# Low parts of the MLP weights: accumulating DMA onto negated high parts in place of a VectorE subtraction

## The chip, the cores and the metric

The kernel runs on one core of one Trainium2 chip. The metric is the device time of one execution in microseconds (us); for the kernel before it is the median of 3 runs.

## The reference

A two-layer decoder trunk over x of 512 tokens by 1024 features, in float32. Layer 0 mixes tokens by differential attention, layer 1 by a chunkwise mLSTM; each mixer is followed by a squared-ReLU MLP, and a final RMSNorm ends it.

```
h = x
for layer in range(DEPTH):                       # DEPTH = 2
    mix = diff_attention(...) if layer % 2 == 0 else mlstm_mixer(...)
    h = h + mix
    h = h + sqrelu_mlp(rmsnorm(h, mlp_norm[layer]), mlp_w1[layer], mlp_w2[layer])
return rmsnorm(h, final_norm)

def sqrelu_mlp(h, w1, w2):                       # w1: 1024 x 4096, w2: 4096 x 1024
    return jnp.square(jax.nn.relu(h @ w1)) @ w2
```

## The kernel before, in words

Activations lie transposed, features on the 128 partitions and the 512 tokens along the row. Every dense product is made of three TensorE passes in a rounded format (fp32r): each operand is split into a high part, its rounded copy, and a low part, the float32 value minus the high part. `mm3` (L296 to L299) issues high x high (L297), high weight x low activation (L298) and low weight x high activation (L299).

The weights are cut into 192 units of 128 x 1024 float32 (two of them 128 x 1056), in the order in which TensorE uses them (`PLAN`). Each entry of `PLAN` is the name of a matrix and its parts; the names are `a_in`, `a_out`, `w1_0`, `w2_0`, `m_in`, `m_out`, `w1_1`, `w2_1`. The two MLPs use 64 units each: for `w1`, four units that serve four output tiles together and 28 of one output tile, for `w2` two units for each of 8 output tiles in each of two halves. A unit is 24 matmuls of 128 x 512.

`issue()` (from L263) brings in one unit. SP issues the load of `raw` from DRAM (L278), ScalarE rounds it into `whi` (through the helper `act`, whose instructions all bear L230), and VectorE subtracts to give `wlo` (L282). `raw`, `whi` and `wlo` have three buffers each. `unit()` is called as TensorE turns to unit u, and issues what is missing up to unit u+2; so the high and low parts of u+2 are written into the buffers that unit u-1 has just left.

TensorE's order is the order of the program, with other work put in at counted steps (`tick`, `after`). The instructions of the other engines are ordered by the scheduler of the language from their dependencies and its own estimates; each engine then runs its instructions in that fixed order and waits where it must.

Around the MLPs the other work is this. At the end of each mixer the output projection (`outproj`) finishes the 8 tiles of h; each is added by VectorE (L499), split by `operand` into `x_xh` (ScalarE) and `x_xl` (VectorE, L409), squared by ScalarE, and the squares are summed into `acc` by GpSimd (L420). Eleven steps into the MLP `token_scale` splits `acc` (L424) and TensorE sums it over partitions (L431, L432). In the `w1` part ScalarE applies Relu, VectorE squares (L754), and both split the result into `u_uh` and `u_ul` (L424). In the `w2` part VectorE scales the result and adds it to h (L766, L767). GpSimd's own DMAs are those of the attention bias (`skew` L533, `bias` L540) and a few constants.

Of the kernel before, what the change touches and what calls it, by code (L numbers as in the profile page):

```python
# [14 lines left out]
AF = mybir.ActivationFunctionType  # L15
ALU = mybir.AluOpType
# [63 lines left out]
def _plan():  # L80

    units = []

    def group(m, cols):
        for k2 in range(KT // 2):
            units.append((m, [(k, c, P) for k in (2 * k2, 2 * k2 + 1) for c in cols]))

    def ntile(m, c, k0=0):
        units.append((m, [(k0 + k, c, P) for k in range(KT)]))

    def vpair(m, c, extra=None):
        for k4 in range(2):
            parts = []
            for k in range(4 * k4, 4 * k4 + 4):
                parts.append((k, c, 256))
                if extra is not None:
                    parts.append((k, extra, 2 * MH))
            units.append((m, parts))

    def outproj(m, wide):  # L100
        order = [(k, n * P, P) for k, n in out_order(wide)]
        units.extend((m, order[i : i + 8]) for i in range(0, len(order), 8))

    def mlp(m1, m2):
        group(m1, [0, P, 2 * P, 3 * P])
        for half in range(2):
            for n in range(16 * half, 16 * half + 16):
                if n >= 4:
                    ntile(m1, n * P)
            for n in range(KT):  # L110
                ntile(m2, n * P, 16 * half)
                ntile(m2, n * P, 16 * half + 8)

    group("a_in", [0, D, P, D + P])
    vpair("a_in", 2 * D)
    for h in range(2, AH):
        ntile("a_in", h * P)
        ntile("a_in", D + h * P)
        if h % 2 == 1 and h < AH - 1:
            vpair("a_in", 2 * D + (h // 2) * 256)  # L120
    vpair("a_in", 2 * D + 3 * 256)
    outproj("a_out", A_WIDE)
    mlp("w1_0", "w2_0")
    vpair("m_in", D, 3 * D)
    for h in range(MH):
        ntile("m_in", h * P)
        ntile("m_in", 512 + h * P)
    for v in range(1, MH):
        vpair("m_in", D + v * 256)
        for n in GATES_AFTER[v]:  # L130
            ntile("m_in", 2 * D + n * P)
    outproj("m_out", M_WIDE)
    mlp("w1_1", "w2_1")
    return units


PLAN = _plan()
# [24 lines left out]
def trunk(ctx: ExitStack, tc, xT, wgt, wgt2, cols, rows, rel, consts, outT):  # L162
    nc = tc.nc
# [10 lines left out]
    def nm(s):  # L174
        return f"{s}_{next(names)}"
# [26 lines left out]
    vec = nc.vector  # L202
    pool = nc.gpsimd

    def asf(t):
        return t.bitcast(F32)
# [5 lines left out]
    def behind(ins, before):  # L212
        tc.add_manual_dep(
            ins.ins, before.ins.name,
            mybir.DependencyInfo(mybir.DependencyClass.NoSync, mybir.DependencyReason.DATA),
            reason="table order",
        )

    def tables(name):
        if loaded["set"] != name:  # L220
            load = nc.scalar.preload_act_table_set(name)
            for use in loaded["uses"]:
                behind(load, use)
            loaded.update(set=name, load=load, uses=[load])

    def act(out, x, func, **kw):
        name = {AF.Exp: LNSET, AF.Ln: LNSET, AF.Sigmoid: SGSET}.get(func)
        if name:
            tables(name)
        ins = nc.scalar.activation(out, x, func, **kw)  # L230
        if name:
            behind(ins, loaded["load"])
            loaded["uses"].append(ins)
# [29 lines left out]
    def issue():  # L263
        u = state["next"]
        state["next"] += 1
        w = WIDTHS[u]
        raw = wp.tile([P, UW], F32, tag="raw", name=nm("raw"))
        if w == 1024:
            src = wgt[u - state["wide"]]
        else:  # L270
            src = wgt2[state["wide"]]
            state["wide"] += 1
        hi = wp.tile([P, UW], F32R, tag="whi", name=nm("whi"))
        lo = wp.tile([P, UW], F32R, tag="wlo", name=nm("wlo"))
        parts = 2 if u < 2 else 1
        for i in range(parts):
            c = slice(i * w // parts, (i + 1) * w // parts)
            nc.sync.dma_start(raw[:, c], src[:, c])  # L278
        for i in range(parts):
            c = slice(i * w // parts, (i + 1) * w // parts)  # L280
            act(hi[:, c], raw[:, c], AF.Copy)
            vec.tensor_tensor(lo[:, c], raw[:, c], asf(hi[:, c]), op=ALU.subtract)  # L282
        ready[u] = (hi, lo)

    used = iter(range(len(PLAN)))
# [1 line left out]
    def ahead(u):  # L287
        while state["next"] <= min(u, len(PLAN) - 1):
            issue()
# [814 lines left out]

    arrive(0)
    issue()
    arrive(1)
    issue()
    for k in range(KT // 2, KT):
        nc.sync.dma_start(h[k], xT[k])  # L1110
# [77 lines left out]
```

## Time and profile before

| | |
|---|---|
| median of 3 runs | 1211.18 us (1209.6 to 1211.62) |
| the profiled execution | 1211.02 us, span 1209.2 us |
| mean granted TensorE clock | 0.992 |
| DMA moved | 111.15 MB, mean 92 GB/s |
| first MLP, second MLP (from the span's start) | 254.6 to 612, 838.7 to 1190 us |

Times within a profile count from the start of its span. PE is TensorE's matmuls, PEld its weight loads, DVE VectorE, ACT ScalarE, POOL GpSimd, SP the engine that issues most DMAs. A row of a group gives line, engine and operation, what is written from what, how often, busy time and mean nanoseconds of one, and then the engine's idle time before them with what ended it. A row of the timeline gives start and duration in us, and in brackets the idle time before it and its releaser. The matmuls are pipelined, so 0.40 us rows start about 0.23 us apart.

### The profile page before, as it was taken

The numbers are of one execution on the slowest core, as the hardware profiler recorded it, in microseconds if no ns is written. First come the engines' busy times: TensorE is split into PE (matmuls) and PEld (weight loads), VectorE is DVE, ScalarE is ACT, GpSimd is POOL, SyncE is SP. The second block draws the span as 40 slices with busy tenths as digits, with TensorE's granted clock in tenths as the row PEclk, the third lists the DMA queues.
The fourth block names the chain that finished last, engine by engine and source line by source line (L and its number), as shares of the span: only waits on it lengthen the run. The fifth ranks groups of instructions, "written<-read, shape, count | busy, mean of one in ns | idle before, by whom it ended". The sixth has DMA issues, their size and how long they took to land.

```text
span 1209.2 us, 14346 instructions
## 1 busy us (share of the span) xinstructions
PE 1175.9 (97%) x5610; PEld 975.0 (81%) x5610; DVE 684.5 (57%) x1063; ACT 524.2 (43%) x845; POOL 168.7 (14%) x157
## 2 busy tenths in 40 slices
PE   8899999999999999999999899999999999999996
PEld 5778888888888888888887789878888888888885
DVE  6789897575433344434469857666544333444444
ACT  5567776454331223433344546655433122433221
POOL 4432332130000000001101312213000000000011
PEclk9999999999999999999999999999999999999998
DMA  6622222222322223232321221222232323222222
GB/s 197 197 70 70 79 79 71 76 99 87 103 89 90 102 87 104 87 103 89 98 93 64 89 69 53 70 87 87 92 100 87 104 88 103 90 91 101 87 70 70
DMA packets 33123, 111.15 MB, mean 92 GB/s; under 512 B 3967, under 2 KB 6034, under 8 KB 33056
## 3 DMA queue, kind: packets, MB, share of 16 engines
q1 hardware_dynamic: 30288, 103.38, 25.9%
q0 software_dynamic: 1648, 5.29, 1.6%
q10 hardware_dynamic: 1120, 1.57, 0.4%
q8 instruction: 44, 0.72, 0.2%
q14 instruction: 23, 0.19, 0.1%
HBM read 108.11 MB, written 4.74 MB: 93 GB/s over the span
## 4 chain that ended last, share of the span: by engine, by line
PE 84%; DVE 8%; ACT 3%; DMA 2%; issue 2%; POOL 1%; DVEq 0%; SPq 0%; ACTq 0%; POOLq 0%
PE bank L298 24%; PE bank L299 24%; PE bank L297 24%; PE bank L330 1%; PE bank L329 1%; PE bank L331 1%; DVE wlo_wlo L282 1%; DMA raw_raw<-wgt 1%; DVE tmp_tmp L827 1%; PE bank L623 1%; PE bank L624 1%; ACT kh_kh L230 1%; PE bank L656 1%; ACT whi_whi L230 1%; DVE e_e L643 0%
## 5 line engine op out<-in xcount | busy, mean ns | idle before, releaser
L282 DVE TENSOR_TENSOR wlo_wlo<-raw_raw,whi_whi 128x1024 fp32r<-128x1024 f32 (+1 forms) x194 | 243.1, 1253 | 269.2 <-ACT whi_whi L230 268.9
L230 ACT ACTIVATE whi_whi<-raw_raw 128x1024 fp32r<-128x1024 f32 (+1 forms) x194 | 203.6, 1049 | 403.4 <-PE bank L298 358.9
L299 PE MATMUL bank<-x_xh,wlo_wlo 128*128 128x512 f32 x768 | 306.0, 398 | 1.1 <-DVE wlo_wlo L282 1.1
L298 PE MATMUL bank<-x_xl,whi_whi 128*128 128x512 f32 x768 | 305.0, 397 | 1.1 <-DVE x_xl L409 1.1
L297 PE MATMUL bank<-x_xh,whi_whi 128*128 128x512 f32 x768 | 303.3, 395 | 2.0 <-ACT whi_whi L230 1.5
L299 PE MATMUL bank<-u_uh,wlo_wlo 128*128 128x512 f32 x496 | 197.1, 397 | 0.0
L298 PE MATMUL bank<-u_ul,whi_whi 128*128 128x512 f32 x496 | 196.3, 396 | 0.0
L297 PE MATMUL bank<-u_uh,whi_whi 128*128 128x512 f32 x496 | 193.7, 391 | 0.0
L297 PEld LDWEIGHTS bank<-x_xh,whi_whi 128*128 128x128 f32 x768 | 146.9, 191 | 35.3 <-ACT whi_whi L230 2.2
L298 PEld LDWEIGHTS bank<-x_xl,whi_whi 128*128 128x128 f32 x768 | 145.0, 189 | 34.3 <-DVE x_xl L409 1.8
L299 PEld LDWEIGHTS bank<-x_xh,wlo_wlo 128*128 128x128 f32 x768 | 144.9, 189 | 34.1 <-DVE wlo_wlo L282 2.1
L420 POOL TENSOR_TENSOR acc_acc<-acc_acc,tmp_tmp 128x512 f32<-128x512 f32 x34 | 53.6, 1576 | 717.8 <-ACT tmp_tmp L230 717.1
L297 PEld LDWEIGHTS bank<-u_uh,whi_whi 128*128 128x128 f32 x496 | 94.6, 191 | 22.0
L298 PEld LDWEIGHTS bank<-u_ul,whi_whi 128*128 128x128 f32 x496 | 93.1, 188 | 22.1
L299 PEld LDWEIGHTS bank<-u_uh,wlo_wlo 128*128 128x128 f32 x496 | 93.1, 188 | 20.2
L766 DVE TENSOR_TENSOR tmp_tmp<-bank,rs_rs 128x512 f32<-128x512 f32 x31 | 21.4, 692 | 107.1 <-PE bank L299 107.1
L230 ACT ACTIVATE u_uh<-tmp_tmp 128x512 fp32r<-128x512 f32 x64 | 40.4, 632 | 79.1 <-DVE tmp_tmp L754 78.9
L329 PE MATMUL bank<-whi_whi,x_xh 128*128 128x256 f32 (+1 forms) x256 | 72.7, 284 | 0.0
L330 PE MATMUL bank<-wlo_wlo,x_xh 128*128 128x256 f32 (+1 forms) x256 | 72.1, 282 | 0.0
L331 PE MATMUL bank<-whi_whi,x_xl 128*128 128x256 f32 (+1 forms) x256 | 72.0, 281 | 0.0
L424 DVE TENSOR_TENSOR u_ul<-tmp_tmp,u_uh 128x512 fp32r<-128x512 f32 x64 | 44.3, 692 | 39.1 <-ACT u_uh L230 39.1
L329 PEld LDWEIGHTS bank<-whi_whi,x_xh 128*128 128x128 f32 x256 | 48.3, 189 | 0.5
(242 smaller groups left out, 1493.3 us busy)
## 6 DMA issues: line engine op xcount, KB each, us to landing
raw_raw<-wgt SPq DMA_DIRECT2D x188, 512.0 KB, 3.5
skew<-frd POOLq DMA_DIRECT2D x8, 320.0 KB, 6.7
bias_bias<-skew POOLq DMA_DIRECT2D x8, 256.0 KB, 3.1
outT<-h SPq DMA_DIRECT2D x6, 256.0 KB, 2.3
raw_raw<-wgt SPq DMA_DIRECT2D x2, 528.0 KB, 3.6
h<-xT ACTq DMA_DIRECT2D x4, 256.0 KB, 6.8
raw_raw<-wgt SPq DMA_DIRECT2D x4, 256.0 KB, 8.7
h<-xT SPq DMA_DIRECT2D x4, 256.0 KB, 6.4
```

The costliest lines, as they stand in the source:

```text
L230: ins = nc.scalar.activation(out, x, func, **kw)
L282: vec.tensor_tensor(lo[:, c], raw[:, c], asf(hi[:, c]), op=ALU.subtract)
L297: mm(ps, whi, x[0], start=first, stop=False)
L298: mm(ps, whi, x[1], start=False, stop=False)
L299: mm(ps, wlo, x[0], start=False, stop=last)
L329: mm(ps, xh, hi[:, c], start=k == 0, stop=False)
L330: mm(ps, xh, lo[:, c], start=False, stop=False)
L331: mm(ps, xl, hi[:, c], start=False, stop=k == KT - 1)
L420: pool.tensor_tensor(acc, acc, s, op=ALU.add)
L424: (eng or vec).tensor_tensor(lo, src, asf(hi), op=ALU.subtract)
L623: mm(ps[m][:, o : o + n], q2[m][:, qs], kh[m][:, :n], start=True, stop=False)
L766: vec.tensor_tensor(y, p, rs2, op=ALU.mult)
```

## The change

In `issue()`, for units whose matrix name begins with "w" (the 128 units of the two MLPs), the subtraction on VectorE is left out. ScalarE makes a second copy of `raw`, with scale -1, into `lo` in the rounded format, and GpSimd issues a DMA that reads the unit's weights again from DRAM and adds them onto `lo`. The other 64 units keep the subtraction.

```
             act(hi[:, c], raw[:, c], AF.Copy)
-            vec.tensor_tensor(lo[:, c], raw[:, c], asf(hi[:, c]), op=ALU.subtract)
+            if PLAN[u][0][0] == "w":
+
+                act(lo[:, c], raw[:, c], AF.Copy, scale=-1.0)
+                nc.gpsimd.dma_start(lo[:, c], src[:, c], accum_op=ALU.add)
+            else:
+                vec.tensor_tensor(lo[:, c], raw[:, c], asf(hi[:, c]), op=ALU.subtract)
         ready[u] = (hi, lo)
```

## Prediction

> **What bounds the kernel now.** I read the page's busy table first, then the table of stretches over the two MLP stages, the costliest groups, the waits of TensorE, and last the timeline of one unit.
>
> ```profile
> PE 1175.9 (97%) x5610; PEld 975.0 (81%) x5610; DVE 684.5 (57%) x1063; ACT 524.2 (43%) x845; POOL 168.7 (14%) x157
> ```
>
> ```profile
> 254.60:612.00 357.40, 357.40 (x1544) 290.79 (x1543) 150.25 (x174) 117.06 (x150) 12.73 (x9) 1.00 0.30 97
> 838.70:1190.00 351.30, 351.30 (x1538) 286.75 (x1537) 149.93 (x171) 110.63 (x141) 10.54 (x7) 1.00 0.27 89
> ```
>
> The second fence holds the two MLP stages; the columns after the length are the busy times of PE, its weight loads, VectorE (DVE), ScalarE (ACT) and GpSimd (POOL), then the granted clock, the DMA share and GB/s. TensorE is busy for the whole of both, 357.40 + 351.30 = 708.7 us, at clock 1.00, while VectorE is busy 300 us of it. In the stages that the change touches, VectorE is not the bound.
>
> ```profile
> L282 DVE TENSOR_TENSOR wlo_wlo<-raw_raw,whi_whi 128x1024 fp32r<-128x1024 f32 (+1 forms) x194 | 243.1, 1253 | 269.2 <-ACT whi_whi L230 268.9
> L230 ACT ACTIVATE whi_whi<-raw_raw 128x1024 fp32r<-128x1024 f32 (+1 forms) x194 | 203.6, 1049 | 403.4 <-PE bank L298 358.9 <-issue 29.0 <-DMA raw_raw<-wgt 7.1
> ```
>
> ```profile
> PE bank L299 <- DVE wlo_wlo L282: 1.1, 2, 0.6
> PE bank L298 <- DVE x_xl L409: 1.1, 2, 0.8
> ```
>
> The 194 subtractions are 192 units, the first two in halves. The second fence is from TensorE's waits over the whole run (us, times, longest): it stood 1.1 us for a low part and 1.1 us for an operand's low part. ACT's 358.9 us of waiting for `L298` is the wait for a buffer: the high part of unit u+2 goes into the buffer that unit u-1 leaves.
>
> ```profile
> 305.24 1.06 ACT L230 ACTIVATE whi_whi<-raw_raw 128x1024 fp32r<-128x1024 f32 x1 [2.03 <-PE bank L298]
> 306.20 0.58 ACT L230 ACTIVATE tmp_tmp<-bank 128x512 f32<-128x512 f32 x1
> 310.78 1.06 ACT L230 ACTIVATE whi_whi<-raw_raw 128x1024 fp32r<-128x1024 f32 x1 [1.96 <-PE bank L298]
> 316.33 1.06 ACT L230 ACTIVATE whi_whi<-raw_raw 128x1024 fp32r<-128x1024 f32 x1 [1.96 <-PE bank L298]
> 306.33 1.23 DVE L282 TENSOR_TENSOR wlo_wlo<-raw_raw,whi_whi 128x1024 fp32r<-128x1024 f32 x1 [2.40 <-ACT whi_whi L230]
> 316.79 0.40 PE L299 MATMUL bank<-x_xh,wlo_wlo 128*128 128x512 f32 x1
> ```
>
> One unit takes 316.33 - 310.78 = 5.55 us. The unit whose high part starts at 305.24 has its low part at 306.33 + 1.23 = 307.56, and TensorE first reads that at 316.79: 9.2 us of slack.
>
> **What is removed.** The MLPs have 2 x 64 = 128 of the 192 units (4 + 28 of `w1` and 32 of `w2` each). 128 subtractions of 1.23 us, 157 us, leave VectorE. None is on the path in the MLP windows, where TensorE had no idle time, so this is worth 0 to 2.2 us (all of both waits above, though nothing shows that they belong to these units). I take 0.
>
> **What ACT gains.** 128 negated copies of the same shape as the high part: 128 x 1.06 = 136 us, on an engine that is busy 117.06 + 110.63 = 228 us of 708.7; it comes to 51%. ACT starts the next instruction 0.96 us after a high part (305.24 to 306.20), so the copy runs from about 306.20 to 307.26, as early as the subtraction ended. The Relu at 306.20 moves back a microsecond, and VectorE's square, which stood behind the subtraction, is free sooner; the result is read a stage later. Cost 0, hidden by TensorE's unit. The raw tile, which the subtraction used to free, is freed by the copy at about the same time, so SP's queue of loads isn't moved.
>
> **What the DMA gains.** Each of the 128 units reads its 512 KB of weights from DRAM a second time and adds them onto the low part in SBUF, issued by POOL. The trace has no accumulating DMA; its nearest rows are POOL's plain loads into SBUF, POOL's copies within DRAM, and SP's loads of this size.
>
> ```profile
> raw_raw<-wgt SPq DMA_DIRECT2D x188, 512.0 KB, 3.5
> skew<-frd POOLq DMA_DIRECT2D x8, 320.0 KB, 6.7
> bias_bias<-skew POOLq DMA_DIRECT2D x8, 256.0 KB, 3.1
> ```
>
> ```profile
> q1 hardware_dynamic: 2592, 9.44, 29.6%
> raw_raw<-wgt SPq DMA_DIRECT2D x18, 512.0 KB, 3.4
> ```
>
> ```profile
> L540 POOL DMA_DIRECT2D bias_bias<-skew x8: 567/590/592, 40.6 to 163.3; - x8
> ```
>
> The last number of the first fence's rows is us from issue to landing; the second fence is the DMA table of the stretch from 300 to 400 us. There 18 loads took 29.6% of 16 engines for 100 us: 29.6 / 18 = 1.64 us of all engines for one 512 KB pass. POOL itself works 0.59 us per issue.
>
> Time to landing, from below: a plain POOL load, 3.1 us for 256 KB and half a pass more, 3.9 us. From above: at the rate of the slowest kind, `skew`, 6.7 x 512 / 320 = 10.7, plus 1.64 for the raw load that the same copy releases and that shares the engines: 12.4 us. An accumulate has to read its destination too, so I take two passes and the raw load beside it: 3.9 + 1.64 + 1.64 = 7.2 us. That is near the `bias` row, which like this one goes from DRAM into SBUF. The DMA may start at 307.26 and is wanted at 316.79, 9.5 us later; 7.2 fits with 2.3 us to spare. Below nothing it can't go, since TensorE has no idle time to give back here.
>
> Engine time: two passes and the raw load are 3 x 1.64 = 4.9 us in a unit of 5.55. It fits as long as the accumulate takes less than 5.55 - 1.64 = 3.9 us, or 2.4 passes. The forecast hangs on this.
>
> The row says 1.64 us for one pass of a copy. The Trainium skill, Collectives: The Full Stack, section "The bandwidth ceiling: the fold count and why AG ≠ RS ≠ AR", holds that a reducing DMA is slower not because of the addition but because it reads two sources, and gives 32.35 against 62.28 GB/s, 1.93 times a copy. By it the accumulate would take an estimated 3.2 us; no run here shows it yet.
>
> **What POOL gains.** A DMA waits in POOL's order for its negated copy, and what stands behind it are the sums of squares (`L420`) that the token scale needs at the start of each MLP.
>
> ```profile
> 243.30 8.76 POOL L420 TENSOR_TENSOR acc_acc<-acc_acc,tmp_tmp 128x512 f32<-128x512 f32 x5 [5.72 <-ACT tmp_tmp L230]
> 245.40 1.05 ACT L230 ACTIVATE whi_whi<-raw_raw 128x1024 fp32r<-128x1024 f32 x1
> 247.47 1.72 DVE L282 TENSOR_TENSOR wlo_wlo<-raw_raw,whi_whi 128x1024 fp32r<-128x1024 f32 x1
> 249.12 3.49 DVE L409 SCALAR_TENSOR_TENSOR x_xl<-h,colt,x_xh 128x512 fp32r<-128x512 f32 x2
> 255.09 0.39 PE L299 MATMUL bank<-x_xh,wlo_wlo 128*128 128x512 f32 x1
> 257.02 1.38 POOL L420 TENSOR_TENSOR acc_acc<-acc_acc,tmp_tmp 128x512 f32<-128x512 f32 x1 [0.86 <-ACT tmp_tmp L230]
> 259.10 0.69 DVE L424 TENSOR_TENSOR sl_sl<-acc_acc,sh_zeros 128x512 fp32r<-128x512 f32 x1 [0.15 <-ACT sh_zeros L230]
> 262.49 0.39 PE L432 MATMUL bank<-sl_sl,ones_d 128*128 128x512 f32 x1
> ```
>
> At the first MLP's start the first unit's high part is at 245.40, its negated copy would end near 247.4, and TensorE reads the low part at 255.09. POOL has five additions in a row there, to 252.06. Between two of them the DMA is issued one addition late, 247.4 + 1.75 = 249.15, and lands 5.5 us (were no raw load beside it) to 7.2 us later, 254.7 to 256.4: a stall of 0 to 1.3 us. Behind all five it lands at 252.06 + 7.2 = 259.3, a stall of 4.2. VectorE's order was planned with this unit's low part ahead of two operands (249.12) that the program names earlier, so work is placed when it is ready; I take the first case, near its upper end because the raw load is released by the same copy: 1 us. The last addition (257.02) may be put off by one issue, 0.6 us, with 262.49 - 259.79 = 2.7 us in hand: 0.
>
> ```profile
> 827.53 1.06 ACT L230 ACTIVATE whi_whi<-raw_raw 128x1024 fp32r<-128x1024 f32 x1 [2.14 <-issue]
> 829.86 1.80 POOL L420 TENSOR_TENSOR acc_acc<-acc_acc,tmp_tmp 128x512 f32<-128x512 f32 x1 [2.82 <-ACT tmp_tmp L230]
> 839.16 0.40 PE L299 MATMUL bank<-x_xh,wlo_wlo 128*128 128x512 f32 x1
> ```
>
> At the second MLP's start the units come more slowly; even behind the addition, at 831.66, a DMA of 7.2 us lands at 838.9, ahead of 839.16: 0.
>
> **Sum.** Removed 0, ACT 0, DMA 0, POOL +1. The profiled execution took 1211.02 us, 1.8 us of it outside its span of 1209.2, and is 0.16 below the median of 1211.18. With +1 the median becomes 1212.2. A measurement of this kernel tells about 0.2% (2.4 us) from no change, so this is no change.
>
> **Rivals.** *The DMA engines become the bound.* For it: nothing here shows an accumulate, three passes in place of two are enough, and the loads come in bursts. Against it: at two passes the engines stay under 90%. It decides from 2.4 passes on. At three passes a unit takes 4 x 1.64 = 6.56 us, 1.01 more than now, times 128: +129 us, 1340. At four it is 1550. With the upper landing bound instead, three units (as many as there are buffers) take copy, DMA and use in turn, (307.26 - 305.24 + 12.4 + 5.55) / 3 = 6.66 us, which is 1.11 x 128 = +142 and 1353.
>
> *POOL's order puts the first DMA behind all five additions.* Steady state hidden, +4.2 at one place: 1215.4. For it: those additions stand earlier in the program. Against it: the VectorE order above.
>
> *VectorE's lighter load frees something.* All of both waits give -2.2 us, 1209.0, still within 0.2%; to be faster than that a chain of VectorE outside the MLPs would have to start sooner. Against it: VectorE is under half busy in both MLPs, so it carries no backlog out of them.
>
> **How the numbers follow.** Forecast, within 2.4 us of before: 0.53, its own range 1209 to 1213.6. DMA engines or landing too slow: 0.31, of which about half is under +142 us. POOL's order: 0.12. Faster by over 0.2%: 0.04. So faster 0.04, same 0.53, slower 0.12 + 0.31 = 0.43. The range from 1208 to 1353 takes in the forecast, POOL's order, half of the slow DMA and most of the rest, 0.83.
>
> **What would show it.** Right: both MLP stretches again with PE busy all of their length, no TensorE wait for the accumulating DMA but at about 255 us, landing near 7 us, DMA share in the MLPs near 0.9. Wrong: TensorE waiting for low parts in every unit, the DMA share near 1.0 (engines) or well below (latency), or a wait of 4 us at the first MLP alone (POOL). The forecast falls if the accumulate takes more than 3.9 us of engine time or lands later than 9.5 us.

## The result, and the profile after

The kernel after takes 1215.45 us (median of 5 runs, 1214.85 to 1216.94) against 1211.18 for the kernel before in the same series (5 runs, 1209.58 to 1212.02). The ratio is 1.0041, with a 95% interval of 1.0026 to 1.0056, some 5 us (the medians differ by 4.3): a small loss, but the whole interval lies beyond the 0.2% that the prediction had set as its border. The profiled execution is the fastest of the five, 1214.85 us, with a span of 1213.1.

The page of the kernel after: busy times, SP's queue with its share of the 16 engines, two groups, and the DMA issues with the us to landing.

```profile
PE 1178.8 (97%) x5610; PEld 976.7 (81%) x5610; DVE 532.8 (44%) x935; ACT 637.6 (53%) x973; POOL 275.3 (23%) x285
...
q1 hardware_dynamic: 30288, 103.38, 29.4%
...
L285 POOL DMA_DIRECT2D wlo_wlo<-wgt x128 | 111.0, 867 | 572.7 <-ACT wlo_wlo L230 555.8
...
L230 ACT ACTIVATE wlo_wlo<-raw_raw 128x1024 fp32r<-128x1024 f32 x128 | 133.9, 1046 | 0.0
...
raw_raw<-wgt SPq DMA_DIRECT2D x188, 512.0 KB, 5.3
wlo_wlo<-wgt POOLq DMA_DIRECT2D x128, 512.0 KB, 7.6
```

The change did what it says: VectorE lost 152 us (684.5 to 532.8), ScalarE gained 113, GpSimd 107. The accumulating DMA lands in a median of 7.6 us, and the plain load beside it now takes 5.3 instead of 3.5. The two MLP stages of the kernel after, with the columns as before:

```profile
254.60:612.00 357.40, 355.69 (x1532) 288.68 (x1532) 76.67 (x110) 171.47 (x212) 65.12 (x72) 1.00 0.87 189
838.70:1190.00 351.30, 351.22 (x1521) 285.69 (x1520) 75.09 (x108) 165.28 (x204) 63.77 (x70) 1.00 0.87 184
```

The DMA share went from 0.30 and 0.27 to 0.87, and TensorE is still busy for nearly the whole of both. Of the first, 1.71 us are missing. TensorE's waits in the kernel after name them:

```profile
PE bank L304 <- DMA wlo_wlo<-wgt: 1.7, 1, 1.7
```

One wait, for one accumulating DMA. Its place is the start of the first MLP; these are rows of the timeline of the kernel after, GpSimd, ScalarE and TensorE:

```profile
244.98 8.22 POOL L425 TENSOR_TENSOR acc_acc<-acc_acc,tmp_tmp 128x512 f32<-128x512 f32 x5 [5.72 <-ACT tmp_tmp L230]
253.14 0.95 POOL L285 DMA_DIRECT2D wlo_wlo<-wgt  x1
...
247.07 1.05 ACT L230 ACTIVATE whi_whi<-raw_raw 128x1024 fp32r<-128x1024 f32 x1
248.03 0.71 ACT L230 ACTIVATE x_xh<-h,colt 128x512 fp32r<-128x512 f32 x1
248.64 0.62 ACT L230 ACTIVATE tmp_tmp<-h 128x512 f32<-128x512 f32 x1
249.27 0.72 ACT L230 ACTIVATE x_xh<-h,colt 128x512 fp32r<-128x512 f32 x1
249.90 0.61 ACT L230 ACTIVATE tmp_tmp<-h 128x512 f32<-128x512 f32 x1
250.42 1.05 ACT L230 ACTIVATE wlo_wlo<-raw_raw 128x1024 fp32r<-128x1024 f32 x1
...
256.30 0.39 PE L302 MATMUL bank<-x_xh,whi_whi 128*128 128x512 f32 x1
...
258.60 0.50 PE L304 MATMUL bank<-x_xh,wlo_wlo 128*128 128x512 f32 x1 [1.68 <-DMA wlo_wlo<-wgt]
```

GpSimd runs all five additions and only then issues the DMA, and ScalarE makes the negated copy four instructions behind the high part. Two matmuls of 0.23 us stand ahead of the first reader, so that was due at 256.30 + 0.47 = 256.77 and came at 258.60, 1.83 us late. The second unit's reader comes another 0.33 us late, found by matching TensorE's instructions of both traces one by one.

The same matching shows 1.65 us of lag by 59 us of the span, long before the first accumulating DMA. It is the clock. In the kernel before:

```profile
28.00:36.00 8.00, 5.62 (x24) 4.03 (x23) 5.21 (x7) 3.48 (x5) 1.92 (x4) 1.00 0.35 106
54.00:64.00 10.00, 9.16 (x39) 7.94 (x40) 7.63 (x28) 4.81 (x18) 1.82 (x3) 0.83 0.35 113
```

and in the kernel after:

```profile
28.00:36.00 8.00, 5.77 (x18) 4.42 (x19) 4.50 (x7) 3.10 (x5) 2.76 (x6) 0.79 0.40 124
54.00:64.00 10.00, 8.76 (x31) 7.65 (x32) 7.44 (x28) 4.70 (x16) 1.79 (x3) 0.66 0.31 107
```

The granted clock, third number from the end, fell to 0.79 and 0.66 over these stretches, where before it was 1.00 and 0.83. So of the 3.9 us between these two spans only 2.2 belong to the change. Whether it costs 2 us in most executions, or the 4 to 5 of the medians and the ratio, was for the experiments to say.

### The profile page after: what moved, and what is told of

Its sections match the earlier page's. It is cut to its first block, busy times and chain, and to the rows that moved or that the text cites. A ratio compares the mean times of both kernels' runs of the same rounds, so it can differ in the third digit from the quotient of the medians.

```text
span 1213.1 us, 14551 instructions
## 1 busy us (share of the span) xinstructions
PE 1178.8 (97%) x5610; PEld 976.7 (81%) x5610; DVE 532.8 (44%) x935; ACT 637.6 (53%) x973; POOL 275.3 (23%) x285
## 3 DMA queue, kind: packets, MB, share of 16 engines
q1 hardware_dynamic: 30288, 103.38, 29.4%
## 4 chain that ended last, share of the span: by engine, by line
PE 82%; DVE 9%; ACT 3%; DMA 3%; issue 2%; POOL 1%; DVEq 0%; SPq 0%; ACTq 0%; POOLq 0%
PE bank L304 24%; PE bank L303 24%; PE bank L302 23%; PE bank L335 1%; PE bank L336 1%; PE bank L334 1%; DVE wlo_wlo L287 1%; DMA raw_raw<-wgt 1%; DVE tmp_tmp L832 1%; DMA wlo_wlo<-wgt 1%; PE bank L628 1%; ACT whi_whi L230 1%; PE bank L629 1%; DVE kl L612 1%; PE bank L661 1%
## 5 line engine op out<-in xcount | busy, mean ns | idle before, releaser
L285 POOL DMA_DIRECT2D wlo_wlo<-wgt x128 | 111.0, 867 | 572.7 <-ACT wlo_wlo L230 555.8
L759 DVE TENSOR_TENSOR tmp_tmp<-tmp_tmp 128x512 f32<-128x512 f32 x64 | 44.3, 692 | 211.8 <-ACT tmp_tmp L230 211.8
L230 ACT ACTIVATE wlo_wlo<-raw_raw 128x1024 fp32r<-128x1024 f32 x128 | 133.9, 1046 | 0.0
L287 DVE TENSOR_TENSOR wlo_wlo<-raw_raw,whi_whi 128x1024 fp32r<-128x1024 f32 (+2 forms) x66 | 86.0, 1303 | 23.5 <-ACT whi_whi L230 23.3
```

The costliest lines, as they stand in the source:

```text
L285: nc.gpsimd.dma_start(lo[:, c], src[:, c], accum_op=ALU.add)
L759: vec.tensor_tensor(r, r, r, op=ALU.mult)
```

## The experiments

All kernels of a series shared their runs of the kernel before; ratios are to those. The median of the kernel before was 1211.18 us in the series of the result and 1211.84, 1211.48 and 1210.90 in the three that follow, which ran on three chips, so kernels of different series are compared by their ratios.

**The kernel before again.** No edit.

> The kernel before, unchanged, timed as if it were a new one. Theory A (the change costs a late first accumulating DMA at the start of the first MLP, 2.2 us in the profile, and the other 1.7 us of the profile's 3.8 are half-clock stretches at the start that come and go): 1211.2, ratio 1.000 within 0.15%, but with spans that scatter by a step of about 1.7 us from run to run. Theory B (the change costs some 2 us spread over the whole run besides the late DMA): 1211.2 with no such steps.

1211.76 us (12 runs), ratio 0.9996 [0.9984, 1.0007]. Its own profile has a granted clock of 1.00 and 0.66 in the two stretches above, where the first profile of the same code had 1.00 and 0.83, and a span of 1211.4 against 1209.2. Two us between single profiles tell nothing here; ratios of many runs and named waits do. The 12 runs are spread from 1208.87 to 1214.17 us with no step among them, so they decide for neither theory.

**The first unit of each MLP subtracted.**

```
-            if PLAN[u][0][0] == "w":
+            if PLAN[u][0][0] == PLAN[u - 1][0][0] == "w":
```

> The first unit of each MLP keeps the subtraction on VectorE, the other 126 use the accumulating DMA. Theory A: TensorE has no wait for an accumulating DMA at the start of the first MLP, and the time falls by 2.2 us against the changed kernel, to 1212 to 1213. Theory B: it falls by 2.2 as well if the late DMA is all that is local, but stays 2 us above before: 1213 to 1214. Rival C (the second unit's DMA is late in its turn, since it also stands behind the additions): the wait only moves by one unit, 1215.

1215.17 us (12 runs), ratio 1.0027 [1.0016, 1.0038]. The wait at the start is gone. Of the 0.41% that the change cost 0.27% are left, 3.3 us: some 1.7 us less, though the two intervals overlap. Theory A, which left nothing or little, missed; Theory B, with 2 us left, is nearest. TensorE's waits, and rows of the timeline, of this kernel:

```profile
PE bank L304 <- DMA wlo_wlo<-wgt: 3.3, 4, 1.3
```

```profile
279.04 0.62 ACT L230 ACTIVATE u_uh<-tmp_tmp 128x512 fp32r<-128x512 f32 x1
279.56 1.06 ACT L230 ACTIVATE wlo_wlo<-raw_raw 128x1024 fp32r<-128x1024 f32 x1
...
280.90 0.86 POOL L285 DMA_DIRECT2D wlo_wlo<-wgt  x1 [7.25 <-ACT wlo_wlo L230]
...
289.11 0.50 PE L304 MATMUL bank<-x_xh,wlo_wlo 128*128 128x512 f32 x1 [1.26 <-DMA wlo_wlo<-wgt]
...
876.47 0.50 PE L304 MATMUL bank<-x_xh,wlo_wlo 128*128 128x512 f32 x1 [1.25 <-DMA wlo_wlo<-wgt]
```

There are four waits where there was one. Two of them are at the same place in both MLPs, the seventh unit, where ScalarE has a backlog of Relu results to split (the first four output tiles end together) and the negated copy stands behind it: the DMA is issued at 280.90 and lands 8.2 us later. The other two (0.25 us at 334 and 0.52 at 541) are single late landings, of 9.1 and 9.9 us.

Were the seventh units' waits new, or had they been there before? These are the DMA and the reader of the first MLP's seventh unit in the kernel after:

```profile
286.11 0.86 POOL L285 DMA_DIRECT2D wlo_wlo<-wgt  x1 [7.24 <-ACT wlo_wlo L230]
...
292.90 0.40 PE L304 MATMUL bank<-x_xh,wlo_wlo 128*128 128x512 f32 x1
```

There the DMA is issued 292.90 - 286.11 = 6.79 us ahead of its reader, which waits for nothing, since it lands after 6.4. In the kernel with the first unit subtracted the reader was due some 6.8 us behind the issue as well (at 287.69, by matching with the kernel before), and the DMA took 8.2. So the wait at the start did not shield this unit: its issue moves with TensorE, and its room stays 6.8 us. What differs is the landing. The profiles of four kernels that have this unit's order as in the kernel after (that one, this one, the sums of squares on VectorE, and the copy ahead in the first unit alone) give eight such cases: all are issued 6.7 to 6.8 us ahead, land after 6.4 to 8.4, and hold TensorE up by 0 to 1.6 us, 0.7 in the mean. The profile of the kernel after, with 0 and 0.24 us, had drawn two of the short ones.

**The sums of squares on VectorE.**

```
-            pool.tensor_tensor(acc, acc, s, op=ALU.add)
+            vec.tensor_tensor(acc, acc, s, op=ALU.add)
```

> The changed kernel with the sums of squares (34 additions) on VectorE instead of GpSimd, so that GpSimd's queue holds nothing ahead of the first accumulating DMA. Theory A: the first DMA is issued when its negated copy ends, near 249, and lands before TensorE needs it near 255: no wait, 1212 to 1213. Rival D (ScalarE's late negated copy, not GpSimd's order, held the DMA): the wait stays, at 1 us or more, 1214 to 1215.

1210.45 us (12 runs), ratio 0.998 [0.9968, 0.9992]. With GpSimd free of additions TensorE has no wait at the start of the first MLP. But its trace also has 4.3 us less by 51 us of the span, in the attention, where the change does nothing, and a wait of 1.47 us at 870, again the seventh unit of the second MLP. So there are two effects in one kernel, and the move has to be tried alone (below). Nor does it part GpSimd's order from ScalarE's (Rival D), since here the scheduler also put the first negated copy directly behind the high part:

```profile
239.61 1.05 ACT L230 ACTIVATE whi_whi<-raw_raw 128x1024 fp32r<-128x1024 f32 x1
240.56 1.04 ACT L230 ACTIVATE wlo_wlo<-raw_raw 128x1024 fp32r<-128x1024 f32 x1
```

**The traffic and the copies without a reader.** The subtraction makes every low part; the negated copy and the DMA go onto a spare tile from the third unit of each MLP on.

```
+            vec.tensor_tensor(lo[:, c], raw[:, c], asf(hi[:, c]), op=ALU.subtract)
+            if PLAN[u][0][0] == "w" and state["spare"]:
+                spare = state["spare"].tile([P, 1024], F32R, tag="spare", name=nm("spare"))
+                act(spare[:, c], raw[:, c], AF.Copy, scale=-1.0)
+                nc.gpsimd.dma_start(spare[:, c], src[:, c], accum_op=ALU.add)
```

> All low parts are made by the subtraction, as before; from the third unit of each MLP on, ScalarE's negated copy and the accumulating DMA run as well, onto a spare tile that nobody reads. This leaves out the gain (the subtraction stays) and keeps the load on ScalarE, GpSimd and the DMA engines. Theory A: nothing waits for the DMA, 1211.2, ratio 1.000. Theory B (ScalarE's extra copies or the DMA traffic slow the rest): 1213 or more.

1212.0 us, ratio 0.9998 [0.9987, 1.0009]. The MLP stages and the landing in this kernel:

```profile
254.60:612.00 357.40, 357.40 (x1542) 290.66 (x1541) 150.55 (x174) 177.16 (x212) 64.96 (x70) 1.00 0.83 187
838.70:1190.00 351.30, 351.30 (x1532) 286.40 (x1531) 146.01 (x170) 169.33 (x200) 62.18 (x68) 1.00 0.81 181
```

```profile
spare_spare<-wgt POOLq DMA_DIRECT2D x124, 512.0 KB, 7.5
```

The DMA engines are as full (0.83 and 0.81) and the landing is as long, and TensorE loses nothing. Neither the traffic, nor the 124 copies on ScalarE, nor GpSimd's issues cost time. The cost is in waiting for the result.

**The sums on VectorE without the change.** The kernel before with the same one-line move.

> The kernel before, with only the sums of squares moved from GpSimd to VectorE; no accumulating DMA. The run with both this move and the change gave 0.998 of the kernel before, with 4.3 us gained by 51 us of its span, ahead of any accumulating DMA. Theory: that gain is of the move alone and the change costs the same 2 to 4 us on top of it as it does without it, through low parts that land late; then this kernel takes 1206.5 to 1208.5 us, 0.996 to 0.997, and is faster than the one with both by 2 to 4 us. Rival 1: with GpSimd free of the additions the change costs nothing; then this kernel takes 1210 to 1211 us, the same as the one with both. Rival 2: the subtractions on VectorE collide with the sums once both are there; then it is above 1212 us, and the change has to be paired with the move to bring anything.

1206.56 us (6 runs, 1204.71 to 1208.23), ratio 0.9962 [0.9949, 0.9974]. The move alone is a gain. The kernel with both stood at 0.998 of its own kernel before, 0.18% or 2.2 us above this one (3.9 by the medians, which are of two series). The intervals just overlap, so that the change costs something with GpSimd free of additions, too, is likely and not shown clear of noise. The profile of that kernel shows 1.5 us of waits for the DMA.

**The negated copy ahead of the high part.**

```
+            if PLAN[u][0][0] == "w":
+                act(lo[:, c], raw[:, c], AF.Copy, scale=-1.0)
+                nc.gpsimd.dma_start(lo[:, c], src[:, c], accum_op=ALU.add)
             act(hi[:, c], raw[:, c], AF.Copy)
-            if PLAN[u][0][0] == "w":
-                act(lo[:, c], raw[:, c], AF.Copy, scale=-1.0)
-                nc.gpsimd.dma_start(lo[:, c], src[:, c], accum_op=ALU.add)
-            else:
+            if PLAN[u][0][0] != "w":
                 vec.tensor_tensor(lo[:, c], raw[:, c], asf(hi[:, c]), op=ALU.subtract)
```

> The kernel after, with the negated copy and the accumulating DMA written ahead of the copy that makes the high part. On GpSimd's queue the first accumulating DMA then stands behind three of the five additions instead of all five, and on ScalarE the negated copy comes one 1.05 us copy earlier at the start of the first MLP. Theory (late low parts at the start of the MLP make the 2.2 us that the profiles show there): the first DMA is issued 2 us or more earlier, the wait of the first reader goes from 1.7 us to below 0.5, and the time comes down by 1.5 to 2.2 us to 1213 to 1214 us, ratio 1.001 to 1.002. Rival A (the cost is single late landings in the middle of the MLPs, which come with the 7.6 us landing and 1.3 us of room): 1215 us, with waits of 1 to 2 us at other units. Rival B (the high part is now the late one): a wait for the high part of some 1 us takes its place, 1215 us or more.

1212.44 us (11 runs, 1209.67 to 1213.34), ratio 1.0001 [0.9993, 1.001]. The cost is gone. Rows of the timeline of this kernel, at the start of the first MLP and at its seventh unit:

```profile
245.38 1.05 ACT L230 ACTIVATE wlo_wlo<-raw_raw 128x1024 fp32r<-128x1024 f32 x1
...
243.28 4.82 POOL L424 TENSOR_TENSOR acc_acc<-acc_acc,tmp_tmp 128x512 f32<-128x512 f32 x3 [5.72 <-ACT tmp_tmp L230]
248.03 0.93 POOL L283 DMA_DIRECT2D wlo_wlo<-wgt  x1
248.65 3.36 POOL L424 TENSOR_TENSOR acc_acc<-acc_acc,tmp_tmp 128x512 f32<-128x512 f32 x2
...
255.06 0.39 PE L303 MATMUL bank<-x_xh,wlo_wlo 128*128 128x512 f32 x1
```

```profile
279.34 1.06 ACT L230 ACTIVATE wlo_wlo<-raw_raw 128x1024 fp32r<-128x1024 f32 x1
...
280.81 1.05 ACT L230 ACTIVATE whi_whi<-raw_raw 128x1024 fp32r<-128x1024 f32 x1
...
280.69 0.86 POOL L283 DMA_DIRECT2D wlo_wlo<-wgt  x1 [5.78 <-ACT wlo_wlo L230]
```

The scheduler now places the first DMA behind three additions, at 248.03; it lands at 253.3, and the reader at 255.06 waits for nothing. At the seventh unit the copy is first after the splits, and its DMA lands after 5.5 us, with 2.8 us of room. In the middle of the MLPs the order on ScalarE is the old one (high part, Relu, negated copy), and the landing has not changed: what its instructions by line say is

```profile
DMA to landing us min/median/max: 5.2/7.7/9.2
```

so the edit works through the two places, not through the steady state.

**Each DMA 2.7 us later.** Two more additions on GpSimd ahead of each DMA from the third unit of each MLP on.

```
+                if state["spare"]:
+                    slow = state["spare"].tile([P, 512], F32, tag="slow", name=nm("slow"))
+                    pool.tensor_tensor(slow, asf(lo[:, :512]), asf(lo[:, 512:1024]), op=ALU.add)
+                    pool.tensor_tensor(slow, asf(lo[:, :512]), slow, op=ALU.add)
                 nc.gpsimd.dma_start(lo[:, c], src[:, c], accum_op=ALU.add)
```

> The kernel after, with two more additions of 128x512 on GpSimd (about 1.35 us each) onto a tile that nothing reads, ahead of each accumulating DMA from the third unit of each MLP on: each DMA is issued some 2.7 us later. Theory (the landing in the steady state has only about 1.3 us of room ahead of its reader): the room is gone in all 124 units; with three buffers a unit's turn round takes the 2.7 us as well, which spread over three units gives 0.25 to 0.42 us a unit, 30 to 52 us in all: 1245 to 1267 us, with waits of TensorE for the accumulating DMA in most units. Rival (the room of 1.3 us is made by the planner and grows when it is needed, since the load can be issued earlier): 1215 to 1218 us.

1239.43 us (4 runs), ratio 1.0219 [1.0196, 1.0242]: some 22 us over the kernel after by the ratios, short of the 30 at least that were expected. The room is thin, as the theory has it, but TensorE waits in 14 places and not in most units: the delay pays part of itself back. Waits, and the landing, of this kernel:

```profile
PE bank L308 <- DMA wlo_wlo<-wgt: 10.5, 14, 3.3
```

```profile
raw_raw<-wgt SPq DMA_DIRECT2D x188, 512.0 KB, 4.5
wlo_wlo<-wgt POOLq DMA_DIRECT2D x128, 512.0 KB, 5.4
```

The copy releases the next plain load too, which used to start 0.3 us ahead of the DMA and now starts 3 us ahead; the DMA lands in 5.4 us instead of 7.6. Of 2.7 us lost at the issue, 2.2 come back at the landing.

**One more plain load of 512 KB for each MLP unit.**

```
+            if PLAN[u][0][0] == "w" and state["spare"]:
+                spare = state["spare"].tile([P, 1024], F32, tag="spare", name=nm("spare"))
+                nc.sync.dma_start(spare[:, c], src[:, c])
```

> The kernel after, with one more plain load of the same 512 KB by SyncE in each unit of the MLPs, onto a tile that nothing reads. In the profile of after the 16 DMA engines are busy for 0.87 of the MLPs, 4.83 us of each 5.55 us unit: 1.64 us for the plain load and 3.2 us for the accumulating one. Theory (that share is time the engines truly hold): one more load makes it 6.47 us a unit, 0.92 us more than TensorE's 5.55, so the MLPs are bound by the DMA engines: 124 times 0.92 is 114 us, 1329 us, with the DMA share at 9 in every slice of the MLPs. Rival (a good part of the 3.2 us is time in which a packet waits for its memory and another could pass): between 1216 and 1260 us.

1295.4 us (4 runs), ratio 1.0689 [1.0674, 1.0704]: 80 us over the kernel after, between the two forecasts. The stretches 254 to 421 and 421 to 640 us of this kernel, and its queues and waits:

```profile
254.00:421.00 167.00, 132.76 (x521) 104.23 (x520) 29.21 (x43) 64.58 (x83) 20.42 (x24) 0.91 0.98 290
421.00:640.00 219.00, 218.69 (x943) 177.52 (x943) 43.29 (x62) 101.13 (x122) 39.85 (x44) 1.00 0.85 186
```

```profile
q1 hardware_dynamic: 48144, 168.40, 38.6%
```

```profile
PE bank L307 <- DMA wlo_wlo<-wgt: 62.2, 19, 8.0
```

In the first stretch the engines are at 0.98 and 290 GB/s, and TensorE is busy for 133 of 167 us; in the second the extra loads are over (SP, with spare tiles that nobody reads, had run ahead: the first MLP's 62 were issued between 212 and 406 us), the share is back at 0.85, and nothing waits. So full engines do hold TensorE up, and the share is a price that is truly paid. The 1.64 us for the added load was too high: 38.6% of 1294.2 us less the 29.4% of 1213.1 us that this queue had in the kernel after is 143 us for 124 loads, 1.15 us each, if the other loads kept their share, which isn't shown. And as the loads came in a burst, the time doesn't tell what one a unit would cost.

**The first and the seventh unit subtracted.**

```
-            if PLAN[u][0][0] == "w":
+            w7 = [PLAN[u - k][0][0] == "w" for k in (0, 1, 6, 7)]
+            if w7[0] and w7[1] and not (w7[2] and not w7[3]):
```

> The kernel after, with the subtraction kept for the first and the seventh unit of each MLP. With the first alone kept the time stayed at 1215.2 us: its profile shows no wait at the start, but 1.3 us at 289 and at 876 us, the seventh unit of each MLP, where the negated copy had come late and two plain loads lay beside the DMA (landing 8.2 us), and single waits at 333 and 540 us. Theory (two places pay: the start of the first MLP and the seventh units; what is left are single late landings): 1212 to 1213.5 us, ratio 1.000 to 1.0015, with no wait at either place. Rival (the single late landings in the middle of the MLPs carry the cost, and where they fall is chance): 1214.5 to 1215.5 us.

1211.44 us (11 runs), ratio 1.0001 [0.9991, 1.0012]. With the first unit alone 3.3 us were left; with the seventh, too, the whole cost is gone. One wait is left in this kernel, in the middle of the second MLP:

```profile
PE bank L305 <- DMA wlo_wlo<-wgt: 0.8, 1, 0.8
```

**The copy ahead in the first unit of each MLP alone.**

```
+            first = PLAN[u][0][0] == "w" and PLAN[u - 1][0][0] != "w"
+            if not first:
+                act(hi[:, c], raw[:, c], AF.Copy)
             if PLAN[u][0][0] == "w":
                 act(lo[:, c], raw[:, c], AF.Copy, scale=-1.0)
                 nc.gpsimd.dma_start(lo[:, c], src[:, c], accum_op=ALU.add)
+                if first:
+                    act(hi[:, c], raw[:, c], AF.Copy)
```

> The kernel after, with the negated copy and its DMA written ahead of the high part for the first unit of each MLP alone; the other 62 units of each stay as they are. Theory (the whole exchange brought 3.0 us, 2.2 of them at the start and the rest at the seventh units): the start's wait goes to below 0.5 us, the one at the seventh units of some 1.3 us each comes up as it did with the first unit subtracted, and the time lies between, 1213 to 1215 us. Rival 1 (the start is all there is): 1212 to 1212.8 us, the same as with the exchange in every unit. Rival 2 (the exchange works in the steady state, by its margins): 1215 us or more.

1214.3 us (11 runs), ratio 1.0021 [1.0012, 1.003], where the theory put it. One detail is otherwise: the first reader waits for nothing, but the second unit's does. Its row, and that of the seventh unit of the second MLP, in this kernel's timeline:

```profile
265.23 0.50 PE L307 MATMUL bank<-x_xh,wlo_wlo 128*128 128x512 f32 x1 [1.49 <-DMA wlo_wlo<-wgt]
...
879.74 0.50 PE L307 MATMUL bank<-x_xh,wlo_wlo 128*128 128x512 f32 x1 [0.60 <-DMA wlo_wlo<-wgt]
```

**Both: the copy ahead and the sums on VectorE.**

> The kernel after with both the negated copy ahead of the high part in every unit and the sums of squares on VectorE. Theory (the exchange takes away what the change costs, and the move of the sums brings its 4.5 us independent of it): 1206.5 to 1208 us, ratio 0.996 to 0.997, the same as the kernel before with the sums moved (1206.6). Rival 1 (with VectorE rid of 128 subtractions of 1.2 us the sums cost it nothing, while in the kernel before they delay something): 1204 to 1206 us, faster than that. Rival 2 (without the additions on GpSimd the exchange has nothing to bring): 1210 us, as with the sums moved alone.

1206.67 us (5 runs, 1205.78 to 1209.03), ratio 0.9961 [0.9949, 0.9974], the same as the kernel before with the sums moved (1206.56). It beats both kernels, but by the move of the sums alone: put right, the change of this case shows no cost and no gain.

## Why the prediction was right or wrong

The time, 1215.45, lies in the range, which was wide, from 1208 to 1353. The forecast itself, 1212.2 and at most 1213.6, was too low. What came is the number of the rival on POOL's order, 1215.4, but by luck: that rival had one stall of 4.2 us, and the runs show several smaller ones.

*What is removed: right.* 152 us less on VectorE moved nothing, since TensorE was busy all through both MLPs. Put right, the change gives 1.0001.

*ScalarE at nothing: the step that failed.* The prediction had the negated copy follow the high part directly, in the MLPs and at their start. In the MLPs the scheduler put it behind the Relu, and this is the steady state of the kernel after:

```profile
309.17 1.06 ACT L230 ACTIVATE whi_whi<-raw_raw 128x1024 fp32r<-128x1024 f32 x1 [2.61 <-issue]
310.13 0.58 ACT L230 ACTIVATE tmp_tmp<-bank 128x512 f32<-128x512 f32 x1
310.61 1.05 ACT L230 ACTIVATE wlo_wlo<-raw_raw 128x1024 fp32r<-128x1024 f32 x1
...
311.95 0.86 POOL L285 DMA_DIRECT2D wlo_wlo<-wgt  x1 [4.75 <-ACT wlo_wlo L230]
```

The DMA starts 2.78 us after the high part where 2.02 were reckoned, and lands in 7.6 where 7.2 were. With 316.79 - 305.24 = 11.55 us from high part to reader, the 2.3 us to spare became 11.55 - 2.78 - 7.6 = 1.2. In most units that is enough. At the seventh, where ScalarE has a backlog and the room for the landing is 6.8 us, and for single landings of up to 9.9 us it is not. The prediction worked out one typical unit and the two MLP starts, and no place inside an MLP where the pattern breaks.

*The DMA engines: right.* 0.87 x 5.55 = 4.83 us of a unit, 4.9 forecast. The added share, 0.57 and 0.60 of 5.55 us, is 3.2 to 3.3 us, about twice the 1.64 of one pass, as taken (the longer time of the plain loads beside it is counted in). By the Trainium skill's rule of two sources (Collectives: The Full Stack, "The bandwidth ceiling: the fold count and why AG ≠ RS ≠ AR"), whose two rates are of collectives (ReduceScatter and AllGather), it was an estimated 3.2, and the trace agrees in size. That a second read is the reason, no run here shows. The 0.31 chance on slow DMAs lay on a limit that is near, as one more load showed, but wasn't reached.

*GpSimd's order: as forecast in length.* The prediction chose between a DMA one addition behind its copy, 1.75 us, and one behind all five, and took the first. It came behind all five, but it waited for no more than one: the negated copy ended at 251.47, as the fourth of five additions of 1.64 us ended (244.98 + 4 x 1.64 = 251.54), and the DMA was issued at 253.14, 1.67 us later. What the step had wrong was the copy, which "would end near 247.4". Of its 4.1 us, 1.7 are the lag that this execution had from the clock, and 2.4 are ScalarE's order: two splits and two squares of other tiles stood between the high part (247.07) and the copy (250.42). The DMA landed in 5.4 us instead of 7.2, so the wait was 1.83 us and not more. With that landing either delay alone would have cost an estimated 0.2 us or nothing: without the addition the DMA lands at 251.47 + 5.4 = 256.9, without the 2.4 us at 256.2, and the reader was due at 256.77.

*The sum.* The prediction had +1 for one place, where there are several: the first two units (2.2 us in the profile) and the seventh of each MLP. By the ratios the change cost 0.41%; with the first unit subtracted 0.27% are left, with the copy ahead in the first unit alone 0.21%, and with both places put right 0.01%. So the first unit carries an estimated 1.7 to 2.4 us, and the seventh units, the second and single late landings the 2.5 to 3.3 us that are left. The profile of the kernel after shows little but the start, because the low parts of its seventh units happened to land early.

*What stays open.* Why the landing at the seventh unit took 6.4 us in one execution and 8.2 to 8.4 in others, with one plain load issued 0.3 us ahead of it and the next some 3.2 us behind it in all of them, isn't shown. The division of the cost is by ratios whose intervals reach 0.1% or more to each side, so it is known to about 1 us. With the sums on VectorE, some 2 us were lost and 1.5 of them were seen as waits.

## What to carry to other kernels

A transfer in place of an on-chip operation adds latency, so cost it at the units where its room is smallest (the start of a stage, the unit after a backlog on the engine that feeds it), not at a typical one. One profile shows one draw of each landing: where the room is smaller than the spread of the landings (6.8 us of room, 6.4 to 8.4 us of landing), a place that doesn't wait in it can still cost time in others, so look at several profiles, or compare ratios of many runs. And when one copy has to start a transfer and the other has not, write the one that starts it first.

## What the runs showed of the hardware

The landing of an accumulating DMA of 512 KB depends on when a plain load of the same size starts beside it: a median of 7.6 us with one issued 0.3 us ahead, 5.4 with that one 3 us ahead, and up to 9.9 in single cases. The plain load pays too, 5.3 us in place of 3.5.

A load's share of the engines is not a constant: the queue of the plain loads held 25.9% of 16 engines for 1209.2 us in the kernel before, 313 us, and 29.4% of 1213.1 us in the kernel after, 357 us, for the same 30288 packets with the accumulating DMAs beside them.

Stretches in which the granted clock drops differ between executions of the same code (0.83 and 0.66 from 54 to 64 us), and two spans of it differed by 2.2 us; between two single profiles that is as much as the first unit's share of the effect looked for.
